# A two-batch transformer encoder on one core: the per-engine instruction order made with another simulated machine

## The chip, the cores and the metric

The kernel runs on one core of one Trainium2 chip. The time is the device time of one execution in microseconds (us). The profile is one execution recorded by the hardware profiler. PE is TensorE's matrix multiplication, PEld its weight load, DVE is VectorE, ACT is ScalarE, POOL is GpSimd, SP is the engine whose queue issues most of the loads. L728 means line 728 of the kernel's file.

## What is computed

Two sequences (512 and 256 tokens, 768 together, width 1024) go through the same two layers. In short:

```
for l in range(DEPTH):
    aq, ak, av, lq, lk, lv, lo, lg = split(x @ w_in[l])
    att  = head_rmsnorm(diff_attention(aq, ak, av, lam, alibi))   # 4 heads
    h    = mlstm_forward(lq, lk, lv, lg) + mlstm_backward(...)    # 4 heads, chunks of 128
    lstm = sigmoid(lo) * head_rmsnorm(h)
    x = layer_norm(ALPHA * x + concat(att, lstm) @ w_out[l])
    gate, up = split(x @ w_gu[l])                                 # 2816 columns each
    x = layer_norm(ALPHA * x + (gelu(conv3(gate)) * up) @ w_down[l])
```

Everything is 32-bit. The large products are split: each operand is a high part (type fp32r) and a low part (the rest), and three products (high by high, high by low, low by high) are summed in PSUM.

## The kernel before, in words

The 768 tokens are six tiles of 128. All of the work is written in one function, `trunk` (L206), once per layer, and the framework turns that text into one list of instructions per engine.

**The mixer.** `lstm_in` (L415) makes the LSTM's q and k and the gates. `gates` (L428) computes the gates' running sums and maxima. `dense` (L397) makes attention's v (av), the LSTM's v (lv) and its output gate (lo), each in six accumulations of 24 matmuls (`tok_major`, L341, issued at L345); `att_in(h)` makes one head's q and k (`feat_major`, L347, issued at L355). `att(h)` (L712) goes through the query tiles of one head: scores (tile s, L728 and L729), then DVE (L730), ACT's exponential (L734), DVE (L735 to L737), PE transposes into tile aT (L740), a copy to SBUF by ACT or DVE in turn (L742), the product with v into tile u (L744), a sum of squares on ACT (L745); after a sequence the norm (POOL's power at L750), the scaling into ao (L752) and transposes aoT (L757). `lstm_states` (L539) and `lstm_out` (L605) do the LSTM, chunk by chunk, in the same manner (tiles ke, cu, kq, qkT, num). `weave` (L760) mixes these generators in the text in fixed proportions.

**The output product and the first norm.** At L898 comes the product with w_out in two halves of columns; the second half is followed per tile by the norm (`layer_norm`, L842), by sums and differences of token tiles (`combine`, L871, on POOL at L880 to L883 or on DVE) and by transposes with a split (`transposed_split`, L358, issued at L362, results at L364 and L365).

**The feed-forward part.** For each of 22 tiles of 128 hidden columns, `ff_tile` (L945) runs seven half-size products (`product`, L937: 12 matmuls of 384 columns at L942) instead of eight (one level of Strassen), combines them on DVE (L958 to L974), convolves (L975 to L978), applies gelu on ACT (L979), multiplies (L980) and splits (L984, L985). After every three tiles (four the last time) `down` (L987) multiplies by w_down: 12 accumulations of 9 (or 12) matmuls of 512 columns at L1002, each added to the residual by DVE at L1009 (the first group at L1007).

**Weights.** Class `Weights` (L95 to L203) loads pieces of 128x512 into six buffers over SP's queue (L140), forms the differences T that Strassen needs (L149, on POOL and DVE), and splits every piece into a high part (ACT, L171) and a low part (DVE, L172); there are twelve pairs of split buffers. `pump` (L177) writes these steps into the text as soon as buffers are named free.

**What sets the order.** The text gives every instruction a priority: its place in the text, moved by the offsets of `prio` (L220; a conversion of weights counts as if it stood 100 places later). PSUM is handed out by tags with a fixed number of banks:

```
BANKS = {"d": 3, "s": 2, "t": 1, "u": 1, "L": 1}
def P(tag, name):
    return pp.tile([128, 512], F32, tag=tag, name=name, bufs=banks[tag])
```

When the `with` block at L1108 ends, the framework's scheduler plays the program on a simulated machine. Whenever a simulated engine takes an instruction, it gets the one with the best priority among those whose inputs and buffers are free at that simulated moment; the order of taking is the order of that engine's list. On the chip the lists are fixed: each engine works through its own and waits by semaphores. So the simulated durations decide which of two instructions stands first; they do not appear in the program in any other way.

Of the kernel before, what the change touches and what calls it, by code (L numbers as in the profile page):

```python
# [1099 lines left out]
def build(arrays, depth=DEPTH):  # L1100
    nc = bacc.Bacc("TRN2", target_bir_lowering=False, num_devices=1, dynamic_dma_scratch_size=1024)
    d = {k: nc.dram_tensor(f"in_{k}_dram", v.shape, F32, kind="ExternalInput").ap() for k, v in arrays.items()}
    o = {"out_0_dram": nc.dram_tensor("out_0_dram", (SA, D), F32, kind="ExternalOutput").ap(),
         "out_1_dram": nc.dram_tensor("out_1_dram", (SB, D), F32, kind="ExternalOutput").ap()}
    d["scr_m"] = nc.dram_tensor("scr_m", (DEPTH, 8, T), F32, kind="Internal").ap()
    d["scr_e"] = nc.dram_tensor("scr_e", (DEPTH, 8, T), F32, kind="Internal").ap()
    d["scr_x"] = nc.dram_tensor("scr_x", (T, D), F32, kind="Internal").ap()
    with tile.TileContext(nc) as tc:  # L1108
        with ExitStack() as ctx:
            trunk(ctx, nc, tc, d, o, depth)  # L1110
    return nc
# [7 lines left out]
```

## Time and profile before

| | us |
|---|---|
| three timed runs | 1816.02, 1815.83, 1812.57 (median 1815.83) |
| the profiled execution | 1814.85 |
| its span, first to last instruction | 1813.1 |
| PE, PEld busy in it | 1772.2, 1575.5 |
| DVE, ACT, POOL busy in it | 1348.4, 774.3, 244.4 |

The profiled execution's time is its span and 1.75 us around it. Busy time of PE is modelled: matmuls are pipelined and overlap in the record, so the space between the starts of two neighbours is the time one takes in a stream, not its own recorded duration. "Idle before" is time in which an engine had nothing running just ahead of the named instruction, with what ended it.

### The profile page before, as it was taken

The page shows a single profiled execution, that of the slowest core. Times are in us where ns is not written, and L with a number is a line of the kernel's source. Part 1 is how long each engine was busy: PE and PEld are TensorE (multiplying, and loading weights), DVE is VectorE, ACT ScalarE, POOL GpSimd, SP SyncE. Part 2 cuts the span into 40 slices and gives each one's busy share as a digit, 9 for nine tenths or more (in the row PEclk, how much of TensorE's full clock was granted, in tenths as well). Part 3 has the DMA queues.
Part 4 walks back from the last instruction along what each step waited for, and adds up shares of the span by engine and source line. Part 5 has one row for each costly group of instructions (what it writes and reads, how often), then busy time and mean ns, then how long its engine had stood idle before and what let it go on. Part 6 is the DMA issues. An engine that isn't in the chain of part 4 may idle for free. (4 is left out here: it accounts for less than half of the span.)

```text
span 1813.1 us, 26263 instructions
## 1 busy us (share of the span) xinstructions
PE 1772.2 (98%) x9692; PEld 1575.5 (87%) x9692; DVE 1348.4 (74%) x2592; ACT 774.3 (43%) x1636; POOL 244.4 (13%) x266
## 2 busy tenths in 40 slices
PE   8999999999999999999999999999999999999998
PEld 8877887889889889899898778878899898898996
DVE  4546887599877787787955468876997787787778
ACT  4445667144334334344233556671453343343340
POOL 2001011141111111110110011101411110111102
PEclk9999999999999999999999999999999999999999
DMA  5312221303122122123232123122122221221211
GB/s 190 100 53 71 76 60 59 139 24 95 57 82 82 47 82 73 56 69 96 94 97 80 53 64 94 47 86 107 37 87 70 65 82 51 78 82 47 82 65 70
DMA packets 89232, 138.09 MB, mean 76 GB/s; under 512 B 7792, under 2 KB 33008, under 8 KB 89104
## 3 DMA queue, kind: packets, MB, share of 16 engines
q1 hardware_dynamic: 88384, 136.05, 23.7%
q8 instruction: 76, 1.25, 0.3%
q14 instruction: 52, 0.43, 0.1%
q10 hardware_dynamic: 720, 0.37, 0.1%
HBM read 130.00 MB, written 6.39 MB: 75 GB/s over the span
## 5 line engine op out<-in xcount | busy, mean ns | idle before, releaser
L942 PE MATMUL p<-actA,wh 128*128 128x384 f32 x1408 | 363.5, 338 | 3.2 <-DVE g L967 3.2
L171 ACT ACTIVATE wh<-raw 128x512 fp32r<-128x512 f32 (+1 forms) x348 | 215.8, 631 | 275.3 <-PE p L942 110.1
L172 DVE TENSOR_TENSOR wl<-raw,wh 128x512 fp32r<-128x512 f32 (+1 forms) x348 | 244.0, 712 | 62.2 <-ACT wh L171 61.7
L942 PE MATMUL p<-actB,wh 128*128 128x384 f32 x1056 | 270.1, 337 | 0.0
L942 PEld LDWEIGHTS p<-actA,wh 128*128 128x128 f32 x1408 | 254.7, 188 | 5.8 <-DVE g L967 3.8
L942 PE MATMUL p<-actA,wl 128*128 128x384 f32 x704 | 237.3, 337 | 0.0
L149 POOL TENSOR_TENSOR T<-raw,raw 128x512 f32<-128x512 f32 x88 | 120.3, 1370 | 837.4 <-DVE wl L172 483.9
L1002 PE MATMUL dn<-wh,actB 128*128 128x512 f32 x576 | 209.1, 396 | 1.4 <-DVE acc L1009 1.4
L171 ACT ACTIVATE wh<-T 128x512 fp32r<-128x512 f32 x176 | 108.5, 629 | 220.6 <-DVE acc L1009 105.3
L942 PEld LDWEIGHTS p<-actB,wh 128*128 128x128 f32 x1056 | 191.2, 188 | 0.0
L1002 PE MATMUL dn<-wh,ring 128*128 128x512 f32 x480 | 179.2, 397 | 1.6 <-DVE acc L1009 1.6
L942 PE MATMUL p<-actB,wl 128*128 128x384 f32 x528 | 177.2, 336 | 0.0
L1009 DVE TENSOR_TENSOR acc<-acc,dn 128x512 f32<-128x512 f32 x144 | 98.3, 683 | 72.2 <-PE dn L1002 72.0
L172 DVE TENSOR_TENSOR wl<-T,wh 128x512 fp32r<-128x512 f32 x176 | 129.8, 749 | 22.1 <-ACT wh L171 22.0
L1002 PEld LDWEIGHTS dn<-wh,actB 128*128 128x128 f32 x576 | 108.0, 188 | 30.3 <-DVE acc L1009 3.4
L942 PEld LDWEIGHTS p<-actA,wl 128*128 128x128 f32 x704 | 132.2, 188 | 0.1
L898 PE MATMUL wo<-wh,actB 128*128 128x512 f32 x384 | 122.9, 397 | 0.0
L1002 PE MATMUL dn<-wl,actB 128*128 128x512 f32 x288 | 113.2, 393 | 0.0
L1002 PEld LDWEIGHTS dn<-wh,ring 128*128 128x128 f32 x480 | 90.0, 188 | 24.6 <-DVE acc L1009 4.2
L942 PEld LDWEIGHTS p<-actB,wl 128*128 128x128 f32 x528 | 99.1, 188 | 0.0
L1002 PE MATMUL dn<-wl,ring 128*128 128x512 f32 x240 | 94.7, 395 | 0.0
L898 PEld LDWEIGHTS wo<-wh,actB 128*128 128x128 f32 x384 | 71.8, 188 | 16.2
(270 smaller groups left out, 3387.9 us busy)
## 6 DMA issues: line engine op xcount, KB each, us to landing
raw<-in_w_g_dram SPq DMA_DIRECT2D x88, 256.0 KB, 2.8
raw<-in_w_u_dram SPq DMA_DIRECT2D x88, 256.0 KB, 2.6
raw<-in_w_down_dram SPq DMA_DIRECT2D x88, 256.0 KB, 2.7
raw<-in_w_out_dram SPq DMA_DIRECT2D x32, 256.0 KB, 2.7
pt<-scr_m SPq DMA_DIRECT2D x12, 512.0 KB, 3.9
qet<-scr_e SPq DMA_DIRECT2D x12, 512.0 KB, 5.2
raw<-in_w_c_dram SPq DMA_DIRECT2D x16, 264.0 KB, 4.0
raw<-in_w_av_dram SPq DMA_DIRECT2D x16, 256.0 KB, 3.5
```

The costliest lines, as they stand in the source:

```text
L149: src["engine"].tensor_tensor(out=src["tile"], in0=a, in1=b, op=ALU.subtract)
L171: self.nc.scalar.activation(h, v, AF.Identity)
L172: self.nc.vector.tensor_tensor(out=l, in0=v, in1=h.bitcast(F32), op=ALU.subtract)
L898: PE.matmul(p, actB[:, k, a, t * 128:(t + 1) * 128], units[k][1 + b], start=n + i == 0, stop=n == 7 and i == 2)
L942: PE.matmul(ps, blk[1 + a][:, k * 128:(k + 1) * 128], x[:, k, b, :], start=k + i == 0, stop=k == 3 and i == 2)
L1002: PE.matmul(p, x, (wh_, wl_)[b], start=k + i == 0, stop=k == nf - 1 and i == 2)
L1009: V.tensor_tensor(out=z, in0=z, in1=p, op=ALU.add)
```

## The change

One argument of the framework's context is set. The scheduler then plays the program on the timeline simulation, the more detailed of the framework's two simulated machines, instead of on the plain model. As the framework describes the two, the plain model leaves out the fixed cost of GpSimd's elementwise instructions; and the timeline simulation keeps, for each engine, a queue of instructions that were taken and have not run. The text of the kernel, the priorities, the buffers, the tags, the engines of all instructions and all constants stay.

```
-    with tile.TileContext(nc) as tc:
+    with tile.TileContext(nc, schedule_with_timeline_sim=True) as tc:
         with ExitStack() as ctx:
             trunk(ctx, nc, tc, d, o, depth)
```

## Rows read from the trace of the kernel before

**Rows 1.** The page: span, and the busy time of each engine.
```profile
span 1813.1 us, 26263 instructions
...
PE 1772.2 (98%) x9692; PEld 1575.5 (87%) x9692; DVE 1348.4 (74%) x2592; ACT 774.3 (43%) x1636; POOL 244.4 (13%) x266
```

**Rows 2.** Busy time by stretch; after the engines the granted clock, DMA share, GB/s.
```profile
core 0: us, PE busy (x) PEld busy (x) DVE busy (x) ACT busy (x) POOL busy (x), PEclk, DMA share, GB/s
0.00:8.00 8.00, 0.70 (x3) 0.70 (x3) 1.59 (x6) 3.38 (x5) 5.23 (x17) 1.00 0.75 228
...
90.00:313.00 223.00, 215.72 (x1307) 179.85 (x1306) 158.93 (x457) 141.71 (x409) 24.00 (x32) 1.00 0.20 61
...
362.00:415.00 53.00, 50.64 (x287) 44.57 (x286) 48.53 (x70) 20.39 (x36) 20.88 (x20) 1.00 0.11 35
415.00:875.00 460.00, 458.40 (x2394) 426.00 (x2394) 364.02 (x596) 180.43 (x294) 51.09 (x38) 1.00 0.24 75
...
990.00:1213.00 223.00, 215.14 (x1303) 178.88 (x1302) 157.31 (x454) 140.53 (x405) 23.15 (x31) 1.00 0.20 60
...
1262.00:1315.00 53.00, 50.68 (x285) 44.29 (x284) 47.77 (x68) 20.15 (x36) 21.84 (x22) 1.00 0.11 35
...
1802.00:1813.10 11.10, 2.96 (x13) 2.06 (x11) 6.51 (x13) 1.66 (x2) 5.63 (x6) 0.74 0.26 94
```

**Rows 3.** Waits of PE from 8 to 1802 us: total, times, longest.
```profile
PE aoT L757 <- DVE ao L752: 3.9, 6, 1.0
PE p L942 <- DVE g L967: 3.2, 2, 1.6
PE s L728 <- ACT sK L705: 3.2, 2, 1.6
PE dn L1002 <- DVE acc L1009: 3.0, 10, 0.6
```

**Rows 4.** Chain of waits, two pieces of the feed-forward part: start, us, what.
```profile
1378.79 44.08 PE p L942 x252
...
1431.49 17.00 PE dn L1002 x72
```

**Rows 5.** Timeline of PE in the first mixer: start, us, instruction.
```profile
246.22 0.28 PE L355 MATMUL aqkB<-actA,wl 128*128 128x256 f32 x1
246.37 0.66 PE L740 MATMUL aT<-ident,tp 128*128 128x128 f32 x4
246.78 0.49 PE L355 MATMUL aqkB<-actA,wh 128*128 128x256 f32 x2
247.11 0.60 PE L592 MATMUL qkT<-ident,hq 128*128 128x128 f32 x4
...
255.32 0.62 PE L355 MATMUL aqkA<-actA,wh 128*128 128x512 f32 x2
255.78 0.39 PE L355 MATMUL aqkA<-actA,wl 128*128 128x512 f32 x1
256.01 0.63 PE L355 MATMUL aqkA<-actA,wh 128*128 128x512 f32 x2
```

**Rows 6.** Tile aT in the first mixer: duration ns min/median/max, first and last start.
```profile
L742 ACT COPY aT<-aT x12: 356/587/591, 109.8 to 306.0; 128x512 f32<-128x512 f32 x8, 128x256 f32<-128x256 f32 x4
L742 DVE COPY aT<-aT x12: 421/682/692, 115.7 to 310.3; 128x512 f32<-128x512 f32 x8, 128x256 f32<-128x256 f32 x4
```

**Rows 7.** Groups on POOL, whole span: busy, mean ns, idle before, releasers.
```profile
L149 POOL TENSOR_TENSOR T<-raw,raw 128x512 f32<-128x512 f32 x88 | 120.3, 1370 | 837.4 <-DVE wl L172 483.9 <-DMA raw<-in_w_u_dram 192.4 <-DVE g L967 87.1
L750 POOL TENSOR_TENSOR ssu<-ssu,mhalf 128x2 f32<-128x2 f32 (+1 forms) x16 | 16.1, 1004 | 142.2 <-DVE ssu L749 142.0
```

**Rows 8.** Groups on DVE from 415 to 875 us.
```profile
L172 DVE TENSOR_TENSOR wl<-raw,wh 128x512 fp32r<-128x512 f32 (+1 forms) x106 | 73.7, 703 | 6.8 <-ACT wh L171 6.8
...
L1009 DVE TENSOR_TENSOR acc<-acc,dn 128x512 f32<-128x512 f32 x60 | 41.0, 683 | 35.4 <-PE dn L1002 35.4
```

**Rows 9.** Timeline of PE at the start.
```profile
7.30 0.60 PE L345 MATMUL c1a<-wh,actA 128*128 128x272 f32 x1 [7.30 <-ACT actA L171]
...
11.18 0.41 PE L345 MATMUL c1b<-wh,actA 128*128 128x256 f32 x1
11.40 0.43 PE L345 MATMUL c1a<-wl,actA 128*128 128x272 f32 x1
...
14.16 0.28 PE L345 MATMUL c1b<-wh,actA 128*128 128x256 f32 x1
14.28 0.28 PE L345 MATMUL c1b<-wl,actA 128*128 128x256 f32 x1
```

## The prediction

> **What bounds the kernel now.** I read the page first: PE is busy for 1772.2 of the span of 1813.1 us [rows 1]. That leaves 40.9 us in which it has nothing running. No instruction is added or removed by the change, and none moves to another engine, so PE's work stays and an order can only alter those 40.9 us, or add to them.
>
> Second, where they lie. The view by stretches gives PE's idle time as stretch less busy [rows 2]: 7.3 us in the first 8, before the first inputs are there; 7.3 us in the first layer's mixer (223 less 215.7) and 7.9 in the second's; 2.4 and 2.3 us around the first norm of each layer; 1.6 us in the 460 us of a feed-forward part; 8.1 us after 1802, behind the last product. The first and last of these are 15.4 us, and hang on the first loads and on the last tile's norm, which every order has at its ends. 25.5 us lie between.
>
> Third, what these 25.5 us are. The largest waits of PE after the start are four kinds of 3 to 4 us each, in pieces of at most 1.6 us, and each for another producer: DVE's ao, g and accumulation, ACT's sK [rows 3]. So there is no single bad place in the order. The wait for ao stands behind POOL's power of 1.0 us (ssu) [rows 7], an elementwise GpSimd instruction, the kind whose fixed cost the plain model leaves out.
>
> Fourth, whether busy PE could go faster with another order. In a piece of chain without any wait, 252 matmuls of 384 columns take 44.08 us, 0.175 each, and 72 of 512 columns 17.00 us, 0.236 each [rows 4]. Nothing waits there, so that is PE's own pace.
>
> The Trainium skill, Perfetto Trace Analysis, section "Identifying the Most-Contended Engine", says that matmul busy time is no good measure of TensorE's headroom and that weight-load busy time is better. By it the headroom would be 1813.1 less 1575.5, some 238 us, against 40.9 by the row. I keep the row's, since the pieces without waits show that the difference is pace; the trace does not bear the rule out as a bound on what an order can win.
>
> **The change, part by part.** Only the order within each engine's list changes. What the rows show of the order of before is that it is made on the spot. In the first mixer PE breaks off an accumulation (aqkB) after a few matmuls, does four transposes of attention (aT), goes on for two, does four of the LSTM (qkT) [rows 5]. An instruction of the long chains (scores, DVE, ACT, DVE, transposes, copy, product) gets in as soon as it is ready in the simulation. That the chip then waits so little (7.3 us of 223) says that the plain model's moments are nearly right there.
>
> *Mixers.* The timeline simulation also takes instructions into queues ahead of their turn. If PE takes the rest of a dense step before the transposes are ready, they stand behind it on the chip too. In each layer attention has 24 steps (12 copies by ACT, 12 by DVE [rows 6]), and each has two PE pieces that follow work elsewhere: the transposes and the product u. The nearest row for the price is one k step of a dense accumulation, three matmuls of 512 columns: 256.01 less 255.32, 0.69 us [rows 5]. Two pieces by 24 steps by 0.69 are 33 us of added chain per layer. Nothing of it shows while PE has dense or LSTM matmuls to do; the mixers have three streams (attention, LSTM, dense products), and I take a third as uncovered, 11 us per layer, because PE is busy 97% of these stretches and the streams end together: what is used as cover early is missing at the end. That third is a choice; its bounds are none (all covered) and all, 66 us for both. The far end, a whole accumulation of 24 matmuls (eight steps, 5.5 us) in front of each piece, I leave out, since the two other streams would then have nothing left to be late for. Below nothing: if every piece of idle time in the two mixers went, 15.2 us would be won. I take +22.
>
> *Around the first norm.* DVE is busy 48.5 of 53 us there and PE idle 2.4 and 2.3. An order that knows POOL's times could win part of the 4.7 us; one that puts weight conversions (0.70 us each [rows 8]) ahead of the norm's steps loses as much. I take nothing.
>
> *Feed-forward parts.* PE idles 1.6 us of 460 and DVE is busy 364, 79% [rows 2]. T on POOL takes 1.37 us but POOL is idle before it for 837 us in total, mostly waiting for DVE's conversions (484) and loads (192) [rows 7], so a right price of POOL finds nothing to repair. I take nothing; what covers a later accumulation is priced under the rivals.
>
> *Start and end.* SP's loads depend on nothing at first and keep the priorities' order; I take nothing, with 2 us either way (a quarter of the first 8).
>
> Sum: 1814.85 and 22 are 1836.9; the profiled execution lies 0.98 us below the median of 1815.83, so against that median it is +1.2%. I forecast **1837 us, slower.** A measurement of this kernel can tell some 0.2% (3.6 us) from no change.
>
> **The rivals.**
>
> *Faster: the better simulated machine places what now waits.* For it: the waits are spread, each a small misjudgement, and POOL's power stands behind the largest kind. Against: 25.5 us is all there is between start and end, and removing some wait in a list fixed beforehand often moves it. Half of it gives 1802, all of it 1789.
>
> *No difference.* Priorities are the same, and if they decide nearly every choice, both simulated machines make nearly the same list, or gains and losses cancel: 1815. Against: the order breaks off accumulations [rows 5], which priorities alone would not do.
>
> *Slower, but in the feed-forward parts.* An accumulation has nine matmuls, 9 by 0.236 or 2.1 us, and two banks take turns, so DVE's addition (0.68 us) may start up to 1.4 us late, two conversions, before PE lacks a bank. If the new list of DVE has three conversions (2.1 us) in front, each addition costs 0.7 us more. With 72 additions that way in each layer, 144 by 0.7 is 100 us, less what PE can do in the next products' six other banks; with a third uncovered as above, 34 us: 1849. Against: 35.4 us of DVE's idle time lies before just these 60 additions [rows 8], so now DVE waits for PE there.
>
> *Slower by the clock.* At the start PE has idled for 7.3 us, and for the first 4 us after it matmuls of 256 to 272 columns follow each other after 0.22 us instead of 0.12 [rows 9], half the pace, so some 2 us are lost, though the granted clock of that stretch reads 1.00; in the last 11.1 us, with PE idle for 8.1, it reads 0.74, a mixture of the two levels of 2.4 and 1.2 GHz. Waits of 1.6 us between leave it at 1.00 [rows 2, 3]. Were the new order to open ten gaps of 5 us, each with such a restart, that would be 10 by 7 us: 1885. The Trainium skill, TensorE: Matmul & The Clock Gate, section "HAM oscillation — how this bites in real kernels", warns of such a cycle of waiting and slow restarts; the trace agrees at its two ends and shows none between. Against it: three streams are there to fill a gap.
>
> **How the numbers follow.** Chances: mixers slower (the forecast) 0.45, feed-forward slower 0.15, clock 0.05, no difference 0.13, faster 0.22. The low end takes in a little over half of the 25.5 us: 1800. The high end is the forecast's full bound, 1814.85 and 66: 1881, which holds the feed-forward rival too. The forecast's own range is 1819 to 1881. Faster 0.22, within 0.2% 0.13, slower 0.65.
>
> **What would show it.** Right: PE's busy time and counts unchanged within 2 us; PE idle in the mixers some 15 to 25 us each instead of 7 to 8; waits of PE for ao, aT, s or num that grow from 1 us to several; accumulations broken off less often; feed-forward stretches as long as before. Wrong: a mixer no longer than 223 us; a wait for the accumulation (dn) or for products' weights that grows in the feed-forward parts; a start that takes longer than 8 us; or all of PE's waits smaller.

## The result and the profile after

The changed kernel takes 1907.30 us (median of four runs, 1905.99 to 1910.43), against 1814.95 us for the kernel before on the same chip: 1.0513 times, 95% interval 1.0495 to 1.0531. The direction was forecast; the size was not, and 1907 lies outside the range of 1800 to 1881. The profiled execution took 1908.29 us, its span is 1906.5.

The page of the kernel after, span, busy time of each engine, and PE's busy share and granted clock in 40 slices:

```profile
span 1906.5 us, 26330 instructions
...
PE 1802.6 (95%) x9692; PEld 1612.6 (85%) x9692; DVE 1359.1 (71%) x2592; ACT 779.2 (41%) x1636; POOL 241.1 (13%) x266
...
PE   8999976889999999999999999778899999999997
...
PEclk9999998898999999999999999989999999999999
```

Against [rows 1]: the same 9692 matmuls, but PE is busy 30.4 us longer (1802.6 less 1772.2) and idle 63.0 us longer (1906.5 less 1802.6 is 103.9, against 40.9). Together that is the whole 93.4 us by which the span grew. The slices show where: two dips, one per layer, each with a lower clock.

To place them I cut both traces at the same events: the first scores (L728), the last transposes aoT (L757), the first product p (L942), the last product dn (L1002). Starts in us, read from the views by line:

| layer | | scores | last aoT | first p | last dn |
|---|---|---|---|---|---|
| 1 | before | 104.4 | 314.5 | 386.3 | 907.3 |
| 1 | after | 104.6 | 365.1 | 431.7 | 954.2 |
| 2 | before | 1004.8 | 1215.9 | 1287.7 | 1804.6 |
| 2 | after | 1050.5 | 1310.2 | 1376.6 | 1896.4 |

The mixers (scores to last aoT) grew from 210.1 to 260.5 us and from 211.1 to 259.7; the stretch from there to the first product shrank from 71.8 to 66.6 and 66.4; the feed-forward parts went from 521.0 to 522.5 and from 516.9 to 519.8; the start is unchanged. The mixer of after also holds some 60 matmuls that came behind it before, 58 of them the output product's, so the two stretches are best taken together: from the first scores to the first product it is 45.2 and 43.1 us more, 88.3 of the 93.4.

The same stretches by busy time, first layer; the kernel before (columns as in [rows 2]: length, then PE, PEld, DVE, ACT and POOL busy, granted clock, DMA share, GB/s):

```profile
104.40:314.50 210.10, 202.55 (x1236) 168.29 (x1235) 152.46 (x448) 135.32 (x394) 22.53 (x28) 1.00 0.19 56
314.50:386.30 71.80, 71.18 (x335) 57.83 (x334) 46.88 (x64) 15.78 (x29) 18.23 (x19) 1.00 0.28 98
```

and the kernel after, with some slices of 25 us out of its mixer:

```profile
104.60:365.10 260.50, 227.10 (x1299) 190.34 (x1297) 158.24 (x453) 137.26 (x396) 20.14 (x28) 0.95 0.16 49
250.00:275.00 25.00, 16.87 (x93) 13.31 (x91) 16.46 (x53) 11.97 (x43) 1.32 (x3) 0.93 0.22 64
...
300.00:325.00 25.00, 14.66 (x80) 12.14 (x79) 15.41 (x53) 11.52 (x37) 3.41 (x5) 0.80 0.23 72
...
365.10:431.70 66.60, 59.91 (x273) 48.66 (x272) 49.62 (x66) 14.97 (x26) 22.96 (x21) 0.94 0.29 103
...
200.00:225.00 25.00, 24.96 (x149) 21.14 (x148) 14.45 (x42) 16.56 (x44) 0.00 (x0) 1.00 0.02 6
```

From 200 to 225 PE has no gap. Behind 250 it is busy 17 and 15 of 25 us in the slices shown, and the granted clock goes down to 0.80. Between lies the end of the largest dense products, attention's q and k: their last matmul (L355) starts at 235.3, where before it started at 278.3. By then attention has issued 72 of its 160 matmuls u in this layer; before, at the end of q and k, it had issued 120:

```profile
L744 PE MATMUL u<-av,aT x72: 270/275/377, 121.5 to 217.5; 128*128 128x128 f32 x72
```

```profile
L744 PE MATMUL u<-av,aT x120: 271/275/377, 110.3 to 266.6; 128*128 128x128 f32 x120
```

(Tile aT, the first of after up to 235.3 us, the second of before up to 278.3.) The LSTM is further behind still. Of its 160 matmuls num, after has issued 24 by 235.3 us; before had issued all 160 by 278.3 (the last at 271.6):

```profile
L636 PE MATMUL num<-vaug,pt x16: 273/275/276, 185.6 to 226.0; 128*128 128x129 f32 x16
L633 PE MATMUL num<-cst,qet x8: 271/273/276, 185.4 to 225.6; 128*128 128x129 f32 x8
```

Of the mixer's own dense work the same is left at that point in both kernels, 72 matmuls of the gate lo (48 of them with wh), but after has 129.8 us of mixer to cover with it (365.1 less 235.3) and before 36.2, besides 66 and 8 matmuls of the output product at the ends. After first, then before:

```profile
L345 PE MATMUL lo<-wh,actA x48: 392/394/502, 235.5 to 298.2; 128*128 128x512 f32 x48
```

```profile
L345 PE MATMUL lo<-wh,actA x48: 388/394/481, 279.3 to 311.9; 128*128 128x512 f32 x48
```

So what is left after 235 us is mostly chains, in which each step waits for another engine. PE's waits in the first mixer, kernel after (total, times, longest):

```profile
PE kq L615 <- DVE hq L648: 4.3, 4, 2.4
PE aT L740 <- DVE hq L648: 3.4, 1, 3.4
PE num L633 <- DVE qz L597: 3.1, 2, 2.5
...
PE qkT L592 <- DVE pt L618: 2.4, 1, 2.4
PE aoT L757 <- ACT hq L647: 2.4, 2, 1.4
PE num L633 <- DVE hq L648: 2.3, 2, 1.5
```

The instructions that end these waits (L597, L618, L647, L648) are all the LSTM's. With one more of this kind (1.0 us) they are 18.9 of the 33.2 us of waits in this mixer. The wait of aT for hq is not for attention's own data: its step's tp was ready at 294.6 us, the transposes start at 307.39, and what they have in common is the one bank of tag t, which aT shares with half of the tiles num.

Why the chains are behind shows, for attention, in the timeline of PE while the dense products last, kernel after (start, us, instruction). The copy of this step's aT to SBUF, on DVE, ends at 207.95:

```profile
207.27 0.68 DVE L742 COPY aT<-aT 128x512 f32<-128x512 f32 x1
```

```profile
206.30 0.60 PE L740 MATMUL aT<-ident,tp 128*128 128x128 f32 x4
206.91 0.51 PE L345 MATMUL lo<-wh,actA 128*128 128x512 f32 x1
207.25 0.40 PE L345 MATMUL lo<-wl,actA 128*128 128x512 f32 x1
207.49 0.63 PE L345 MATMUL lo<-wh,actA 128*128 128x512 f32 x2
...
211.66 0.62 PE L345 MATMUL lo<-wh,actA 128*128 128x512 f32 x2
212.12 0.40 PE L345 MATMUL lo<-wl,actA 128*128 128x512 f32 x1
212.36 1.05 PE L744 MATMUL u<-av,aT 128*128 128x128 f32 x8
```

The product u starts at 212.36, 4.41 us after its data are there, and PE never paused: 23 matmuls of the gate lo stand between the transposes and u in its list, all but one of the accumulation's 24. In [rows 5] two matmuls stand between such pieces.

### The profile page after: what moved, and what is told of

Same layout as the page of the kernel before. It is cut to its first block, busy times and chain, and to the rows that moved or that the text cites. A ratio compares the mean times of both kernels' runs of the same rounds, so it can differ in the third digit from the quotient of the medians.

```text
span 1906.5 us, 26330 instructions
## 1 busy us (share of the span) xinstructions
PE 1802.6 (95%) x9692; PEld 1612.6 (85%) x9692; DVE 1359.1 (71%) x2592; ACT 779.2 (41%) x1636; POOL 241.1 (13%) x266
## 5 line engine op out<-in xcount | busy, mean ns | idle before, releaser
L942 PE MATMUL p<-actA,wh 128*128 128x384 f32 x1408 | 366.9, 341 | 0.2
L942 PE MATMUL p<-actB,wh 128*128 128x384 f32 x1056 | 273.8, 338 | 0.2 <-ACT actB L364 0.2
L942 PEld LDWEIGHTS p<-actA,wh 128*128 128x128 f32 x1408 | 259.7, 190 | 5.4 <-ACT actA L364 0.7
L942 PE MATMUL p<-actA,wl 128*128 128x384 f32 x704 | 238.8, 339 | 0.0
L1002 PE MATMUL dn<-wh,actB 128*128 128x512 f32 x576 | 207.8, 394 | 0.0
L942 PEld LDWEIGHTS p<-actB,wh 128*128 128x128 f32 x1056 | 192.6, 188 | 4.4 <-ACT actB L364 0.7
L1002 PE MATMUL dn<-wh,ring 128*128 128x512 f32 x480 | 178.0, 395 | 0.6 <-DVE acc L1009 0.6
L942 PE MATMUL p<-actB,wl 128*128 128x384 f32 x528 | 177.9, 337 | 0.0
L1009 DVE TENSOR_TENSOR acc<-acc,dn 128x512 f32<-128x512 f32 x144 | 98.2, 684 | 89.2 <-PE dn L1002 88.3
L898 PE MATMUL wo<-wh,actB 128*128 128x512 f32 x384 | 129.3, 413 | 9.1 <-ACT actB L364 6.2
L942 PEld LDWEIGHTS p<-actA,wl 128*128 128x128 f32 x704 | 133.5, 190 | 1.1
L1002 PEld LDWEIGHTS dn<-wh,actB 128*128 128x128 f32 x576 | 108.2, 188 | 23.1
L172 DVE TENSOR_TENSOR wl<-T,wh 128x512 fp32r<-128x512 f32 x176 | 117.5, 683 | 5.2 <-ACT wh L171 5.2
L1002 PE MATMUL dn<-wl,actB 128*128 128x512 f32 x288 | 113.4, 394 | 0.0
L1002 PEld LDWEIGHTS dn<-wh,ring 128*128 128x128 f32 x480 | 90.0, 188 | 20.2 <-DVE acc L1009 1.5
L942 PEld LDWEIGHTS p<-actB,wl 128*128 128x128 f32 x528 | 99.2, 188 | 0.5
L1002 PE MATMUL dn<-wl,ring 128*128 128x512 f32 x240 | 94.7, 395 | 0.0
## 6 DMA issues: line engine op xcount, KB each, us to landing
raw<-in_w_c_dram SPq DMA_DIRECT2D x16, 264.0 KB, 3.9
```

Of the source, the lines that this page charges most:

```text
L172: self.nc.vector.tensor_tensor(out=l, in0=v, in1=h.bitcast(F32), op=ALU.subtract)
L898: PE.matmul(p, actB[:, k, a, t * 128:(t + 1) * 128], units[k][1 + b], start=n + i == 0, stop=n == 7 and i == 2)
L942: PE.matmul(ps, blk[1 + a][:, k * 128:(k + 1) * 128], x[:, k, b, :], start=k + i == 0, stop=k == 3 and i == 2)
L1002: PE.matmul(p, x, (wh_, wl_)[b], start=k + i == 0, stop=k == nf - 1 and i == 2)
L1009: V.tensor_tensor(out=z, in0=z, in1=p, op=ALU.add)
```

## The experiments

Each experiment is the kernel of after with the edit shown, but for one that says so. Most edits are to settings of the simulated machine, which decide the order and reach the chip in no other way. The theory that the first runs start from (Q): the timeline simulation lets TensorE take many ready instructions ahead into its queue, so whole dense accumulations get in front of attention's pieces. Rivals: the queues of the other engines do it (D), or the price of GpSimd's instructions (G).

**TensorE's queue cut to four places.**

```
TRN2Spec.ENG_ISSUE_QUEUE_DEPTH = {**TRN2Spec.ENG_ISSUE_QUEUE_DEPTH, ET.PE: 4}
```

> Edit: the timeline simulation's queue for TensorE is cut to 4 places; everything else as in the changed kernel. Theory Q (TensorE's simulated queue lets dense matmuls be taken ahead of attention's and the LSTM's steps, so that the dense work is used up early and the chains run on alone): most of the 92 us goes; the mixers lose some 15 us each instead of 47, total 1835 to 1855, TensorE idle in the stretch from the first scores to the last aoT well below the changed kernel's. Theory G (GpSimd's fixed cost, now priced, reorders the work) and theory D (queues of VectorE, ScalarE and GpSimd): no change from 1907, within 10 us.

Measured: 1835.11 us, 1.0118 times before (1.0103 to 1.0133). Over three quarters of the loss (92.4 us, now 21.1) are gone with this one number.

**TensorE's queue cut to one place** (`ET.PE: 1` in the same line).

> Edit: TensorE's simulated queue cut to 1 place. Theory Q: chain pieces are again placed when they become ready; total 1810 to 1835, mixers within 10 us of the kernel before. Theories G and D: still near 1907.

Measured: 2282.26 us, 1.2581 (1.2562 to 1.26): far off, and worse than after. This needed a reason of its own, below.

**The other engines' queues cut to one place.**

```
TRN2Spec.ENG_ISSUE_QUEUE_DEPTH = {**TRN2Spec.ENG_ISSUE_QUEUE_DEPTH, ET.DVE: 1, ET.Activation: 1, ET.Pool: 1}
```

> Edit: the simulated queues of VectorE, ScalarE and GpSimd cut to 1 place, TensorE's left as it is. Theory D (conversions of weights taken into VectorE's and ScalarE's queues delay the chains): most of the 92 us goes, below 1850. Theories Q and G: 1895 to 1915.

Measured: 1901.38 us, 1.0483 (1.0468 to 1.0499), some 6 us better than after. D falls as the main cause.

**GpSimd's fixed costs taken out again.**

```
TRN2Spec.GPSIMD_OP_FIXED_NS_AND_CYCLES_PER_ELEMENT = {}
TRN2Spec.GPSIMD_TENSOR_TENSOR_READ_CYCLES = (0, 0, 0)
TRN2Spec.GPSIMD_TENSOR_SCALAR_OP_CYCLES = (0, 0, 0)
```

> Edit: the timeline simulation's own costs of GpSimd's elementwise instructions are emptied, queues left as they are. Theory G: returns most of the way to 1815. Theories Q and D: 1895 to 1915.

Measured: 1908.14 us, 1.0515 (1.0498 to 1.0533), the same as after. G falls.

**Twelve places and two places.** If Q holds, harm must grow with the number of places. Where an expectation speaks of R, that is the explanation of the run with one place, taken up again as S below.

> Edit: TensorE's simulated queue cut to 12 places. Theory Q: between 4 places (1835) and the full queue (1907), 1860 to 1885, and the last aoT of the first layer between 330 and 365 us. If only the very short queue matters (some other effect of it than run-ahead), it stays at 1900 or above.

> Edit: TensorE's simulated queue cut to 2 places. Theory Q alone: 1815 to 1835, a little below 4 places. Theory R (a queue of 1 gave 2282 because a queue too short to overlap weight loads with products also makes the simulated TensorE too slow, so that everything else is placed as if TensorE were late): 2 places already show some of that, above 1850, with waits for VectorE in the feed-forward parts.

Measured: 1856.98 us, 1.024 (1.021 to 1.0269), 3 us under what was expected; and 1828.32 us, 1.0082 (1.0052 to 1.0111), as Q expected; R asked for over 1850, so it isn't seen at two places. The first mixers of two, four and twelve places, in this order, by busy time (columns as above):

```profile
107.40:323.60 216.20, 212.82 (x1298) 181.22 (x1297) 155.26 (x452) 135.41 (x396) 21.68 (x28) 1.00 0.19 59
```

```profile
106.50:330.50 224.00, 215.67 (x1298) 184.24 (x1297) 155.76 (x452) 135.25 (x396) 22.38 (x28) 0.98 0.19 57
```

```profile
108.60:342.30 233.70, 218.05 (x1298) 186.54 (x1297) 157.54 (x452) 136.21 (x396) 21.53 (x28) 0.96 0.17 54
```

The kernel before has 62 matmuls fewer in this stretch and those 62 more behind it, so the fair length is from the scores to the first product. With it, two delays of an attention step, each as the median of the layer's first 12 steps and worked out from the timelines: from the end of tp (L737) to the start of its transposes, and from the end of the copy (L742) to the start of its u. The last column is how many of the 160 matmuls u and of the 160 matmuls num had been issued when the last one of q and k (L355) started:

| places | us | scores to first p | tp to aT | copy to u | PE idle in mixer | clock in mixer | u, num by then |
|---|---|---|---|---|---|---|---|
| plain model | 1814 | 281.9 | 0.2 | 0.14 | 7.6 | 1.00 | 120, 160 |
| 2 | 1828 | 278.4 | 1.1 | 0.54 | 3.4 | 1.00 | 96, 112 |
| 4 | 1835 | 286.0 | 1.4 | 0.79 | 8.3 | 0.98 | 88, 104 |
| 12 | 1857 | 297.5 | 2.3 | 1.65 | 15.7 | 0.96 | 80, 72 |
| as the change has it | 1907 | 327.1 | 6.4 | 4.18 | 33.4 | 0.95 | 72, 24 |

Within the timeline simulation everything follows the number of places, the LSTM's progress above all. With two, the mixer with its norm is even 3.5 us shorter than before.

**The chains first, on the timeline simulation.** Do priorities cure it?

```
-PR_A = 0
-PR_L = 0
+PR_A = 400
+PR_L = 400
```

> Edit: the changed kernel with the priorities of attention and of the LSTM raised by 400 places (PR_A and PR_L from 0 to 400). Theory Q: no cure, since a chain's next piece isn't ready when the dense matmuls are taken: 1890 to 1925. Theory P (it is a matter of priorities that were set for the other order): a large part comes back, below 1860.

Measured: 1917.19 us, 1.0572 (1.0541 to 1.0602), 10 us worse than after. Priorities don't cure it, and P falls. Q's reason, that a better number doesn't help an instruction that isn't ready when the queue is filled, agrees with this but was not tested by itself.

**The chains late, on the plain model.** The same harm without the change: before, with attention and LSTM numbered 1000 places later.

```
-PR_A = 0
-PR_L = 0
+PR_A = -1000
+PR_L = -1000
```

> Edit: the kernel before, plain model, with the priorities of attention and of the LSTM lowered by 1000 places, so that ready dense matmuls go first there too. Theory Q: the same harm without the timeline simulation, though smaller since a piece that is ready waits for no queue: mixers 10 to 40 us longer each, 1835 to 1895. If dense work placed early does no harm by itself: within 6 us of 1815.

Measured: 1869.21 us, 1.0307 (1.0269 to 1.0345). Its first scores start at 132.3 instead of 104.4, its q and k (L355) end at 264.0 instead of 278.3, and its first mixer is

```profile
132.30:350.30 218.00, 196.52 (x1179) 163.27 (x1177) 150.35 (x443) 127.56 (x372) 21.48 (x28) 0.98 0.17 54
```

with 21.5 us of PE idle. From the scores to the first product it takes 281.9 us, as before, so what it loses is the 27.9 us by which the chains began late, once per layer; copy to u stays at 0.1 us. The mixers themselves were expected to grow by 10 to 40 us and grew by 7.9 and 4.2. All 144 matmuls of lv now stand ahead of the scores, 120 of which were in the mixer before, and yet the way from the scores to the first product got no shorter. So the harm doesn't need the timeline simulation: dense work done early is missing as cover later. It doesn't repeat the detail of after, where the chains begin on time and are held up on the way.

**What made one place so bad?** Its waits of PE over the whole span:

```profile
PE dn L1002 <- DVE acc L1009: 84.0, 10, 8.9
PE aT L740 <- DVE tp L737: 77.0, 28, 11.1
```

The first was 3.0 us in [rows 3]. The theory S: with one place the simulated TensorE becomes too slow, and everything else is placed as if PE were late. Four places again, and a simulated pass of at least 400 ns:

```
TRN2Spec.ENG_ISSUE_QUEUE_DEPTH = {**TRN2Spec.ENG_ISSUE_QUEUE_DEPTH, ET.PE: 4}
TRN2Spec.PE_MIN_PASS_INTERVAL_NS = 400.0
```

> The run with one place in TensorE's simulated queue took 2282 us where I expected 1810 to 1835. Theory S: there the simulated TensorE became too slow (each instruction waits for the one before), so the scheduler believed that VectorE and ScalarE had time to spare, and put other work ahead of the copies and additions that the real TensorE waits for. Test: four places again (1835.1 us), but every simulated pass of TensorE takes at least 400 ns, about twice what the trace shows (0.175 to 0.236 us). By S: over 2000 us, near 2282, feed-forward parts much longer than 522 us per layer, with the waits for acc and tp at the head of TensorE's list as in that run. Rival T (one place is special in some way of its own, and the speed of the simulated matmul doesn't matter): 1825 to 1850.

Measured: 2207.65 us, 1.2168 (1.215 to 1.2186). T falls, and what S forecast came: a slow simulated TensorE is enough for such a loss. That one place works in this way is inferred from the same waits. The first feed-forward part takes 587.3 us (514.3 to 1101.6) instead of 521.0, the second 582.0 instead of 516.9. The larger share of the loss lies in the mixers, though: from the scores to the first product it is 405.0 and 403.5 us, against 281.9 and 282.9 before. The waits are of the same two kinds:

```profile
PE dn L1002 <- DVE acc L1009: 64.2, 10, 6.7
PE aT L740 <- DVE tp L737: 39.8, 24, 6.4
```

One of them, in the timelines of PE and then of DVE:

```profile
749.87 0.40 PE L1002 MATMUL dn<-wh,actB 128*128 128x512 f32 x1
756.94 0.80 PE L1002 MATMUL dn<-wh,ring 128*128 128x512 f32 x1 [6.67 <-DVE acc L1009]
```

```profile
750.52 1.51 DVE L172 TENSOR_TENSOR wl<-T,wh 128x512 fp32r<-128x512 f32 x1
751.95 0.94 DVE L980 TENSOR_TENSOR up<-up,c 128x768 f32<-128x768 f32 x1
754.06 0.69 DVE L149 TENSOR_TENSOR T<-raw,T 128x512 f32<-128x512 f32 x1 [1.16 <-POOL T L149]
754.67 1.02 DVE L985 TENSOR_TENSOR actB<-up,actB 128x384 fp32r<-128x384 f32 x2
755.60 0.68 DVE L149 TENSOR_TENSOR T<-T,raw 128x512 f32<-128x512 f32 x1
756.21 1.27 DVE L1009 TENSOR_TENSOR acc<-acc,dn 128x512 f32<-128x512 f32 x2
```

PE's last matmul before the gap starts at 749.87, but DVE's list has a conversion, a product, differences and the split of a finished tile ahead of the additions that free the banks; by S, because in the simulation the accumulations ended much later. DVE even idles 1.16 us for POOL meanwhile. That is what the forecast's rival of a slower feed-forward part described.

**Three tries at a better version**, each with two places. Where two places still lose, by the starts of scores, first p and last dn (107.4, 385.8, 913.8 and 1011.5, 1289.1, 1814.4): start 3.0 us, feed-forward 7.0 and 8.4; they win 3.5 and 5.3 from the scores to the first product. The edits: `VT = ()`, `VT = (4, 5)` instead of `(5,)` (which token tiles' `combine`, L878, runs on DVE; the expectations call that a norm), and `PR_LO = -60` instead of 10 (most of lv, lo and the LSTM's splits, 70 places later).

> Two places in TensorE's simulated queue (1828.3 us) left three new costs against the kernel before: start and gates +3, mixers about +6 each, feed-forward about +7 each; its norm stretch was some 10 us shorter. Here also no token tile's norm is on VectorE (VT empty instead of tile 5), all on GpSimd. If VectorE is what the last tile waits for: 1815 to 1826. If GpSimd then ends last in the norm stretch: 1830 to 1850.

> Two places again, and two token tiles' norms on VectorE (4 and 5). If GpSimd sets the end of the norm stretch: 1818 to 1827. If VectorE, busy nine tenths of that stretch, does: 1830 to 1845.

> Two places again, and the dense products of the mixer get the priority number -60 instead of 10. Theory Q has the remaining 6 us per mixer in dense matmuls that are taken ahead of attention; by it another priority moves the time by under 8 us either way, since what is ready is taken at once whatever its number (1820 to 1836), as the run with the chain's priorities first showed. By rival P (priorities decide nearly every choice) the mixers change by over 20 us each, to 1860 or more or to under 1810.

Measured: 1830.51 us (1.007 to 1.0102 times before), 1826.62 (1.0053 to 1.0083) and 1835.14 (1.0096 to 1.013). The first two can't be told from plain two places (1.0052 to 1.0111), so which engine combines these tiles isn't what is in the way; the third stays within what Q allows, and P falls. None beats the kernel before. What costs two places their 7 and 8 us in the feed-forward parts stays open.

## Why the prediction was right and wrong

**Right: the mechanism and its place.** "If PE takes the rest of a dense step before the transposes are ready, they stand behind it on the chip too" is what the timeline of after shows, and the harm falls with the number of places from 1907 to 1857, 1835 and 1828. Feed-forward at nothing measured +1.5 and +2.9 us; the start at nothing, 0.2. The waits for num and aT, at most 0.4 us in the first mixer before, grew to 2.5 and 3.4 us, as said would show it. The stretch around the norm, also at nothing, was 5 us shorter, but only because 58 matmuls of the output product were done in the mixer. At the forecast's 0.236 us each [rows 4] they are 13.7 us, so by this estimate it lost over 8.

**Wrong: the price of a piece.** The step that failed is "Two pieces by 24 steps by 0.69", with one k step of three matmuls ahead of each piece. Measured, by the medians of the table, the transposes came 6.2 us and the product u 4.0 us later than before, nine and six times as much. That is about the "whole accumulation of 24 matmuls" of 5.5 us, which was named as the far end and left out. Over the 48 pieces of the first layer the delays sum to 358.4 us against 48.1. The delays of neighbouring steps overlap, so this sum is not time; the time in which at least one piece was ready and not started, behind other work or for want of a bank, is 201.1 us against 43.6. That is 157.5 us more per layer, where the forecast had 33. I had no row for how far ahead the simulation takes, took the nearest, and dropped the far end on an argument, so the range could not hold the result.

**Wrong: the argument for dropping it.** It said that the two other streams would "then have nothing left to be late for". The dense products did run down early: q and k ended at 235.3 us instead of 278.3, and the 72 matmuls of lo that remained had over three times as long a stretch to cover. The LSTM did not run out; it was late itself, with 24 of 160 matmuls num issued by then, and over half of the waits in the mixer end with its instructions. The forecast counted it as cover alone and put its own pieces at nothing, without a reason.

**The third.** The share taken as uncovered was not far off: 45.2 us (scores to first product, 327.1 less 281.9) of 157.5 is 29%. With the measured delay the forecast's own sum would have been 1814.85 plus twice 157.5 by a third, 1920, 12 us above the profiled 1908. That it comes so near is partly luck, since the cover isn't a fixed share. With two places the held-up time is 108.4 us, 64.8 more than before, and all of it is covered; from there to after 92.7 more cost 48.7 (327.1 less 278.4).

**Wrong: PE's busy time.** "PE's busy time and counts unchanged within 2 us" held for the counts; the busy time was 30.4 us off. The clock rival, at 0.05, is part of the result: at two places 1298 matmuls of the first mixer keep PE busy for 212.8 us at a clock of 1.00, in after 1299 take 227.1 at 0.95. Of the 44.3 us between those two mixers (260.5 less 216.2) 14.3 are longer busy time and 30.0 are idle time. The lower level was granted in four stretches of this mixer (columns as above):

```profile
260.15:263.56 3.41, 3.19 (x15) 2.89 (x15) 1.23 (x7) 1.39 (x8) 0.00 (x0) 0.50 0.11 35
304.52:314.76 10.24, 6.69 (x26) 6.02 (x27) 6.50 (x17) 3.40 (x10) 1.20 (x2) 0.50 0.18 66
325.00:331.83 6.83, 4.87 (x14) 3.90 (x15) 6.41 (x12) 4.14 (x9) 1.97 (x2) 0.50 0.01 2
355.72:362.55 6.83, 5.20 (x19) 4.14 (x20) 2.70 (x6) 2.27 (x5) 0.99 (x1) 0.50 0.01 2
```

PE is busy for 20.0 us in them; at half pace some 10 of the 14.3 us are the clock's (an estimate), and the rest is not explained. The rival had asked for gaps of 5 us; no wait of PE in this mixer is over 3.4. How much of the 10 us would have been waited for anyway wasn't separated. The forecast's reading of 1.00 at the start is an empty one: the trace of before has no clock record ahead of 11.9 us, which lies between the half and the full pace of [rows 9].

**Right: the faster rivals' weakness.** 25.5 us were to be had at most, and no order tried here beat the kernel before. Pricing GpSimd gave nothing (1908 without it, 1907 with it).

## What to carry to other kernels

A scheduling simulation is judged by which instruction it lets stand first, not by how much detail it has: where an engine may take ready work far ahead, the filler that should cover a chain is spent before the chain has steps to cover, and afterwards the engine waits mostly for the chain. If the simulation has such a depth, bound its effect by whole units of filler (here an accumulation of 24 matmuls, 5.5 us) rather than by the smallest, and look at when the filler runs out. Ask of each stream that you count as cover whether it is a chain itself: here the LSTM was, and it fell furthest behind. The opposite error costs more: with simulated matmuls too slow, other engines put other work ahead of what PE waits for (2208 and 2282 us), so the bottleneck's simulated pace should be checked against its pace in the trace [rows 4] first.

## What was unexpected of the hardware

The granted clock of TensorE fell inside a kernel, with no wait of PE over 3.4 us: in the stretch from 300 to 325 us PE was busy 14.66 of 25 us, and the clock reads 0.80, a mixture of the levels of 2.4 and 1.2 GHz. The timeline of after shows the same eight matmuls u at either level:

```profile
309.18 2.08 PE L744 MATMUL u<-av,aT 128*128 128x128 f32 x8 [0.68 <-ACT aT L742]
```

against 1.05 us at 212.36 above. So the slower TensorE lengthens steps of the very chain it waits for. In the run with one place, whose waits in the first mixer reach 11.1 us, the first mixer's clock reads 0.82.
